# Holding back residual loads until an attention map has been turned: a two-layer hybrid encoder on one core

## The chip, the cores and the metric

The kernel runs on one core of a Trainium2 chip. The metric is the time of one execution in device microseconds (us). Times are medians of a few runs of the same program. The rows shown come from one profiled execution.

## The reference

Two layers over 512 tokens of width 1024, in float32. Each layer computes

```
xn  = RMSNorm(x) * g0
mix = [ A(xn) | B(xn) | C(xn) ] @ w_out        # one input projection, three mixers
h   = x + RMSNorm(mix) * g1
y   = h + RMSNorm( convFFN( RMSNorm(h) * g2 ) ) * g3
```

A is a mixture of dilated window attentions (4 heads), B a bidirectional gated linear recurrence computed in chunks (4 heads), and C is differential attention: 4 heads, each with two query/key maps of 64 dims and values of 128 dims, dense over the sequence; the second softmax is subtracted from the first with a learned weight, and the result goes through an RMSNorm. Queries and keys of A and C get a partial rotation. The convFFN projects to 2 x 2816 columns, runs a convolution of width 3 along the tokens, gates one half with the SiLU of the other and projects back to 1024.

## The kernel before, in words

Each float32 operand of a product is split into a rounded part and a remainder, and a product is three matmuls (`prod`). Weights come in tiles of 128 x 1024 floats (512 KB) into three buffers (`raw`); ScalarE or VectorE makes the rounded part, VectorE the remainder (the subtraction), and only then is the buffer free for the next load. Activations live as four row tiles of 128 tokens, or transposed ("turned") as eight k-slices of 128 features by 512 tokens, again in two parts.

One layer goes: the input projection in chunks, interleaved with the mixers (`mixer`, in the order of `STEPS`); the mixers' results are turned into `xm`, slices 0 to 3 for A and B (`turn_ab`) and slice 4 + h for head h of C (`turn_c`), where head 1 is turned first; the output projection from `xm`; for each row tile the post norm, which adds the residual `x` (`post_norm`), and the second norm, whose result is turned into `xn` (`norm_in`); then the FFN (`ffn`), whose convolution weights stand in `conv`.

For each pair of maps of A and C, `queries_keys` projects queries and keys, multiplies them by cosines and sines on VectorE, lets GpSimd issue four small DMAs that add the swapped rows, splits the result, and lets GpSimd issue twelve DMAs ("moves", 128 KB each, SBUF to SBUF) that put both halves of queries and keys where the score matmuls read them: eight for the queries' two parts and four for the keys, in the order first half, second half.

All loads from HBM (weights, row tiles, norm weight rows, convolution weights) are issued by SyncE, whose queue is in order: an instruction that waits for its buffer holds all that stand behind it. GpSimd issues the moves.

The order of each engine's instructions is made by a planner (`Plan.order`). Every instruction is recorded with its readers and writers; the planner keeps a clock for each engine and, whenever an engine is free, takes the ready instruction with the lowest number, where weight loads and their splits have theirs lowered by 1875 (`AHEAD`). A result is usable on another engine 200 ns after it ends (2000 ns for a DMA). Buffers share their places with others by stage, and an instruction can be taken only when its buffer has a place. What is issued is the resulting order; semaphores on the chip follow from the data that instructions really share. `once` adds views to what the planner takes an instruction to read, and to nothing else:

```python
    def once(self, *views):
        self.needs.extend(views)
        yield
        del self.needs[-len(views):]
```

The planner's prices, in ns for n elements per partition, of VectorE, ScalarE (plus 93 for each view that it takes as scale, bias or accumulator) and DMAs, and what it adds (40 on VectorE, 20 on ScalarE); a DMA keeps SyncE for its price:

```python
            return 68 + n / (1.92 if fast else 0.96) + 61 * scalar
            return (112 if src else 155) + n / 1.4 + 93 * extra + (61 if n > 512 else 0)
        return math.prod(out.shape) * 4 / 350.0
            cost = op.cost + MORE.get(e, 0)
                free[e] = t + (max(50, op.cost) if e == "sync" else 785)
```

Of the kernel before, what the change touches and what calls it, by code (L numbers as in the profile page):

```python
# [21 lines left out]
NT, NK = 4, 8  # L22
# [494 lines left out]
class Trunk:  # L517
# [544 lines left out]
    def layer(self, l, xs):  # L1062
        nc = self.nc
        if l == 0:
            self.first_constants()
            self.xn = self.x_tiles("x%d" % (l % 2))
            rows = [self.t([128, D], "x") for _ in range(NT)]
            with nc.ahead(6 * AHEAD):
                nc.sync.dma_start(rows[0], xs[0])
                g = self.gain_halves()  # L1070
            for t in range(1, NT):
                with nc.ahead((5 if t == 1 else 2) * AHEAD):
                    nc.sync.dma_start(rows[t], xs[t])
            for t in range(NT):
                with nc.ahead((3 if t < 2 else 0) * AHEAD):
                    self.norm_in(rows[t], g, t, self.xn)
            with nc.ahead(-LATER):
                self.constants()
        self.mixer(l)
        self.x = [self.t([128, D], "x") for _ in range(NT)]  # L1080
        g1, g2 = self.gain(l, 1), self.gain(l, 2)
        for t in range(NT):
            nc.sync.dma_start(self.x[t], xs[t])
        self.xn = self.x_tiles("x%d" % (1 - l % 2))
        first = [self.bank("mm") for _ in range(NT)]

        def token(out, q, t, w):
            for i in range(2):
                k = 2 * q + i
                self.prod(out, [z[:, k, t * 128:(t + 1) * 128] for z in self.xm],  # L1090
                          [z[:, i * 512:(i + 1) * 512] for z in w], k == 0, k == NK - 1)

        for q in range(4):
            w = self.weight(l, BASE["out"] + 2 * q)
            for t in range(NT):
                token(first[t], q, t, w)
        ws = [self.weight(l, BASE["out"] + 2 * q + 1) for q in range(4)]
        for t in range(NT):
            second = self.bank("cp")
            for q in range(4):  # L1100
                token(second, q, t, ws[q])
            with nc.ahead(NORM):
                self.post_norm([first[t], second], self.x[t], g1)
                self.norm_in(self.x[t], g2, t, self.xn)
        self.ffn(l)
# [35 lines left out]
    def ffn(self, l):  # L1141
        nc = self.nc
        v = nc.vector
        y = [self.t([128, D], "y") for _ in range(NT)]
        self.conv = self.t([128, 2 * NJ, 4], "conv")
        nc.sync.dma_start(self.conv, self.a["conv"][:, l])
        groups = [(0, 8), (8, 16)]
        jobs = [(a, b, half, q) for a, b in groups for half in range(2) for q in range(a // 2, b // 2)]
        hs = {}
        ps = None  # L1150
        done = 0

        def piece(a, b, half, q):
            nonlocal ps
            first, last = q == a // 2, q == b // 2 - 1
            if first:
                ps = [self.bank("dn") for _ in range(NT)]
            self.down(l, hs, q, half, ps, range(NT), first, last)
            if last:
                for t in range(NT):  # L1160
                    yt = y[t][:, half * 512:(half + 1) * 512]
                    if a == 0:
                        nc.copy(yt, ps[t])
                    else:
                        v.tensor_tensor(yt, ps[t], yt, op=ALU.add)

        start = [[self.bank("mm") for _ in range(2)] for _ in range(2)]
        for lo in (0, 256):
            for j in range(2):
                self.up(l, j, start[j], lo, lo + 256)  # L1170
        for j in range(NJ):
            if j < 2:
                u = start[j]
            else:
                u = [self.bank("mm") for _ in range(2)]
                self.up(l, j, u)
            hs[j] = self.gate(l, j, u)
            if done < len(jobs) and jobs[done][1] <= j:
                piece(*jobs[done])
                done += 1  # L1180
        for job in jobs[done:]:
            piece(*job)
        g1 = self.gain(l, 3)
        last = l == L - 1
        if not last:
            g2 = self.gain(l + 1, 0)
        ws = {(half, q): self.weight(l, BASE["down"] + 2 * q + half, tag="v%d" % (l % 2) if (half, q) == V_TILE else "w")
              for half in range(2) for q in range(8, 11)}
        if not last:
            self.xn = self.x_tiles("x%d" % (1 - l % 2))  # L1190
        for t in range(NT):
            both = [self.bank("cp" if t == 2 else "mm") for _ in range(2)]
            for half in range(2):
                for q in range(8, 11):
                    self.down(l, hs, q, half, [both[half]], (t,), q == 8, q == 10, ws[half, q])
            ys = [y[t][:, half * 512:(half + 1) * 512] for half in range(2)]
            with nc.ahead(NORM):
                for yt, p in zip(ys, both):
                    v.tensor_tensor(yt, p, yt, op=ALU.add)
                self.post_norm(ys, self.x[t], g1)  # L1200
            if last:
                for half in range(2):
                    h = slice(half * 512, (half + 1) * 512)
                    nc.sync.dma_start(self.a["out"][0, t * 128:(t + 1) * 128, h], self.x[t][:, h])
            else:
                nc.sync.dma_start(self.spill[t], self.x[t])
                with nc.ahead(NORM):
                    self.norm_in(self.x[t], g2, t, self.xn)


WB = 5
V_TILE = (1, 10)


# [9 lines left out]
def lay_out(plan, pool, psum):  # L1224
# [6 lines left out]

    rsize, fsize = (64 + 8 * WB) * K, 86 * K
    rtile = pool.tile([128, rsize], F32R, name="rounded")
# [4 lines left out]
    def place(arena, size, at, tags):  # L1238
        for name, n, bufs in tags:
            at = plan.tag(name, arena, at, n, bufs)  # L1240

        assert at <= size, (at, size)
        return at

    base = place(ra, rsize, 0, (("whi", 4 * K, WB), ("wlo", 4 * K, WB)))
    for side in ("0", "1"):
# [58 lines left out]
```

## Time and profile before

| | |
|---|---|
| median of 3 runs | 1390.62 us (1389.17 to 1391.64) |
| the profiled execution | 1389.02 us, with a span of 1387.3 us |
| TensorE's granted clock, mean | 0.998 of full |
| busy share of the span | TensorE 98%, VectorE 69%, ScalarE 50%, GpSimd 12% |
| loads on SyncE's queue | 129.37 MB, 29.2% of the 16 DMA engines' time |
| GpSimd's DMAs | 20.47 MB, 6.4% |

Busy time is summed over the span; the stretch around the change has its own table below. Nearly every instruction is recorded through one helper, so all carry the same line, L514, and are told apart by engine, operation, shapes and place in time. "full" is the float32 area that holds many tiles, "rounded" the area of split operands, "bank" PSUM; w_d, x_d, gains_d and conv_d are the inputs in HBM, "spill" the store of the first layer's result, from which the second layer loads its residual.

### The profile page before, as it was taken

The page shows a single profiled execution, that of the slowest core. Times are in us where ns is not written, and L with a number is a line of the kernel's source. Part 1 is how long each engine was busy: PE and PEld are TensorE (multiplying, and loading weights), DVE is VectorE, ACT ScalarE, POOL GpSimd, SP SyncE. Part 2 cuts the span into 40 slices and gives each one's busy share as a digit, 9 for nine tenths or more (in the row PEclk, how much of TensorE's full clock was granted, in tenths as well). Part 3 has the DMA queues.
Part 4 walks back from the last instruction along what each step waited for, and adds up shares of the span by engine and source line. Part 5 has one row for each costly group of instructions (what it writes and reads, how often), then busy time and mean ns, then how long its engine had stood idle before and what let it go on. Part 6 is the DMA issues. An engine that isn't in the chain of part 4 may idle for free.

```text
span 1387.3 us, 19687 instructions
## 1 busy us (share of the span) xinstructions
PE 1361.5 (98%) x7462; PEld 1165.5 (84%) x7462; DVE 957.4 (69%) x1655; ACT 695.7 (50%) x1171; POOL 160.8 (12%) x263
## 2 busy tenths in 40 slices
PE   8999999999999999999999999999999999999997
PEld 6998889877888888888899888897888888888885
DVE  6789999858765455445768899997586644554374
ACT  4837875645543334323356576756464433343231
POOL 1031332311000000000111132333010000000000
PEclk9999999999999999999999999999999999999999
DMA  7343442623523223223253343355153332332311
GB/s 249 122 112 101 113 112 72 174 75 100 174 92 100 98 91 106 93 94 104 72 179 97 119 117 99 84 145 137 46 158 116 95 103 92 101 97 91 107 62 61
DMA packets 46159, 151.10 MB, mean 109 GB/s; under 512 B 7920, under 2 KB 8432, under 8 KB 46064
## 3 DMA queue, kind: packets, MB, share of 16 engines
q1 hardware_dynamic: 37584, 129.37, 29.2%
q0 software_dynamic: 8480, 20.47, 6.4%
q8 instruction: 59, 0.97, 0.3%
q14 instruction: 36, 0.29, 0.1%
HBM read 125.17 MB, written 4.19 MB: 93 GB/s over the span
## 4 chain that ended last, share of the span: by engine, by line
PE 92%; DVE 4%; issue 1%; ACT 1%; DMA 1%; POOL 1%; DVEq 0%; POOLq 0%; ACTq 0%
PE bank L514 92%; DVE full L514 2%; DVE rounded L514 1%; ACT full L514 1%; POOL full L514 1%; DMA full<-full 0%; ACT rounded L514 0%; DMA full<-gains_d 0%; DVE qz L514 0%; DVEq L1275 0%; POOLq L1275 0%; DVEq L514 0%; POOL ident masks.py:197 0%; ACTq L514 0%; POOLq masks.py:199 0%
## 5 line engine op out<-in xcount | busy, mean ns | idle before, releaser
L514 PE MATMUL bank<-rounded 128*128 128x512 f32 (+1 forms) x5904 | 1218.3, 363 | 2.4 <-DVE rounded L514 1.6
L514 PEld LDWEIGHTS bank<-rounded 128*128 128x128 f32 x5904 | 992.7, 189 | 166.4 <-ACT rounded L514 2.5
L514 DVE TENSOR_TENSOR rounded<-full,rounded 128x1024 fp32r<-128x1024 f32 (+2 forms) x268 | 294.1, 1110 | 210.4 <-ACT rounded L514 204.9
L514 ACT ACTIVATE rounded<-full 128x1024 fp32r<-128x1024 f32 (+2 forms) x241 | 237.3, 987 | 366.3 <-PE bank L514 328.3
L514 ACT ACTIVATE full<-full 128x512 f32<-128x512 f32 (+7 forms) x335 | 183.6, 568 | 108.8 <-DVE full L514 96.2
L514 ACT ACTIVATE full<-bank,full 128x512 f32<-128x512 f32 (+1 forms) x182 | 121.5, 673 | 119.0 <-PE bank L514 78.0
L514 DVE SCALAR_TENSOR_TENSOR full<-bank,full 128x511 f32<-128x511 f32 x176 | 130.4, 747 | 50.9 <-ACT full L514 48.1
L514 DVE TENSOR_TENSOR full<-full 128x256 f32<-128x256 f32 (+2 forms) x265 | 146.7, 573 | 12.5 <-ACT full L514 4.1
L514 POOL TENSOR_TENSOR full<-full,half 128x1 f32<-128x1 f32 (+1 forms) x48 | 45.0, 939 | 903.0 <-DVE full L514 903.0
L514 ACT ACTIVATE full<-bank 128x512 f32<-128x512 f32 (+2 forms) x160 | 89.6, 574 | 42.6 <-PE bank L514 34.4
L514 PE MATMUL bank<-full 128*128 128x128 f32 (+2 forms) x640 | 82.4, 297 | 3.6 <-ACT full L514 3.6
L514 PEld LDWEIGHTS bank<-full 128*128 128x128 f32 (+1 forms) x640 | 72.4, 180 | 15.3 <-ACT full L514 7.3
L514 POOL DMA_DIRECT2D rounded<-full x144 | 75.1, 533 | 50.0 <-ACT full L514 33.4
L514 DVE SCALAR_TENSOR_TENSOR full<-full 128x512 f32<-128x512 f32 (+1 forms) x100 | 71.9, 738 | 10.6 <-POOL full L514 10.0
L514 PE MATMUL bank<-ident,full 128*128 128x128 f32 x464 | 72.1, 279 | 5.3 <-DVE full L514 5.2
L514 POOL DMA_DIRECT2D full<-full x48 | 41.2, 1248 | 258.6 <-DVE full L514 258.6
L514 PEld LDWEIGHTS bank<-ident,full 128*128 128x128 f32 x464 | 56.3, 143 | 17.0 <-DVE full L514 10.4
L514 PE MATMUL bank<-qz,full 128*128 128x128 f32 x448 | 63.4, 282 | 0.6 <-DVE full L514 0.2
L514 PEld LDWEIGHTS bank<-qz,full 128*128 128x128 f32 x448 | 58.0, 190 | 7.1 <-DVE full L514 4.7
L514 DVE TENSOR_TENSOR full<-bank,full 128x512 f32<-128x512 f32 (+1 forms) x56 | 35.9, 648 | 25.4 <-PE bank L514 25.2
L514 DVE TENSOR_TENSOR qz<-full 64x256 f32<-64x256 f32 x112 | 46.6, 416 | 4.8 <-PE bank L514 2.5
L514 DVE TENSOR_REDUCE full<-bank 128x1 f32<-128x512 f32 x64 | 43.7, 685 | 5.5 <-PE bank L514 4.3
(59 smaller groups left out, 369.5 us busy)
## 6 DMA issues: line engine op xcount, KB each, us to landing
full<-w_d SPq DMA_DIRECT2D x204, 512.0 KB, 3.5
rounded<-full POOLq DMA_DIRECT2D x144, 128.0 KB, 4.0
full<-w_d SPq DMA_DIRECT2D x16, 384.0 KB, 3.2
full<-x_d SPq DMA_DIRECT2D x8, 512.0 KB, 4.4
full<-gains_d SPq DMA_DIRECT2D x7, 512.0 KB, 4.6
spill<-full SPq DMA_DIRECT2D x4, 512.0 KB, 2.8
full<-spill SPq DMA_DIRECT2D x4, 512.0 KB, 5.3
out_d<-full SPq DMA_DIRECT2D x8, 256.0 KB, 2.0
```

The lines of the kernel that those rows point to most:

```text
L514: f(*[real(v) for v in op.args], **{k: real(v) for k, v in op.kw.items()})
```

## The change

Two places get a `once`. The loads of two norm weight rows (`g1`, `g2`) and of the four row tiles of the residual are, for the planner, readers of slice 5 of `xm`'s rounded part, which `turn_c` writes for head 1, the second map of kind C. The load of the convolution weights is a reader of the first 128 tokens of `xn`, which `norm_in` writes for the first row tile.

```diff
@@ layer
         self.mixer(l)
         self.x = [self.t([128, D], "x") for _ in range(NT)]
-        g1, g2 = self.gain(l, 1), self.gain(l, 2)
-        for t in range(NT):
-            nc.sync.dma_start(self.x[t], xs[t])
+        with nc.once(self.xm[0][:, LAST_MAP]):
+            g1, g2 = self.gain(l, 1), self.gain(l, 2)
+            for t in range(NT):
+                nc.sync.dma_start(self.x[t], xs[t])
@@ ffn
         self.conv = self.t([128, 2 * NJ, 4], "conv")
-        nc.sync.dma_start(self.conv, self.a["conv"][:, l])
+        with nc.once(self.xn[0][:, :, 0:128]):
+            nc.sync.dma_start(self.conv, self.a["conv"][:, l])
@@
 WB = 5
+LAST_MAP = 5
 V_TILE = (1, 10)
```

## Rows read from the trace of the kernel before

**Rows 1.** The page, parts 1 and 4: busy time, and the chain by engine.
```profile
PE 1361.5 (98%) x7462; PEld 1165.5 (84%) x7462; DVE 957.4 (69%) x1655; ACT 695.7 (50%) x1171; POOL 160.8 (12%) x263
...
PE 92%; DVE 4%; issue 1%; ACT 1%; DMA 1%; POOL 1%; DVEq 0%; POOLq 0%; ACTq 0%
```

**Rows 2.** Busy time by stretch, both layers.
```profile
core 0: us, PE busy (x) PEld busy (x) DVE busy (x) ACT busy (x) POOL busy (x), PEclk, DMA share, GB/s
...
230.00:262.00 32.00, 32.00 (x213) 28.57 (x212) 26.63 (x51) 18.70 (x40) 11.95 (x18) 1.00 0.57 158
262.00:285.00 23.00, 21.14 (x120) 17.41 (x118) 17.54 (x34) 13.76 (x31) 10.53 (x17) 1.00 0.67 186
285.00:330.00 45.00, 44.30 (x226) 36.67 (x226) 28.81 (x54) 23.65 (x55) 5.14 (x7) 1.00 0.16 47
...
944.00:967.00 23.00, 20.88 (x119) 17.15 (x117) 17.28 (x35) 13.76 (x31) 10.54 (x17) 1.00 0.69 185
```

**Rows 3.** SyncE's queue in order of time: start, duration.
```profile
230.55 0.33 SPq L514 DMA_DIRECT2D full<-gains_d  x1
...
245.59 0.33 SPq L514 DMA_DIRECT2D full<-x_d  x1
...
260.64 0.33 SPq L514 DMA_DIRECT2D full<-w_d  x1
261.07 1.60 SPq L514 DMA_DIRECT2D full<-x_d  x2
271.90 25.49 SPq L514 DMA_DIRECT2D full<-w_d  x3
```

**Rows 4.** TensorE in order of time, 280 to 286 us; idle time in brackets.
```profile
280.62 1.16 PE L514 MATMUL bank<-full 128*128 128x128 f32 x8 [1.13 <-ACT full L514]
...
284.25 0.71 PE L514 MATMUL bank<-rounded 128*128 128x512 f32 x2
285.27 2.11 PE L514 MATMUL bank<-rounded 128*128 128x512 f32 x8 [0.31 <-ACT rounded L514]
```

**Rows 5.** ScalarE in order of time, 262 to 287 us.
```profile
268.27 0.69 ACT L514 ACTIVATE rounded<-bank,dnorm 128x512 fp32r<-128x512 f32 x1 [1.26 <-PE bank L514]
...
271.13 0.64 ACT L514 ACTIVATE full<-full 128x512 fp32r<-128x512 f32 x1
```

**Rows 6.** VectorE in order of time, around 270 and 311 us.
```profile
270.65 1.22 DVE L514 TENSOR_TENSOR rounded<-full,rounded 128x1024 fp32r<-128x1024 f32 x1
...
311.50 0.69 DVE L514 TENSOR_TENSOR full<-bank,full 128x512 f32<-128x512 f32 x1 [0.83 <-PE bank L514]
```

**Rows 7.** GpSimd in order of time: issues of the moves.
```profile
272.06 4.17 POOL L514 DMA_DIRECT2D rounded<-full  x8 [3.39 <-ACT full L514]
277.83 2.15 POOL L514 DMA_DIRECT2D rounded<-full  x4 [1.60 <-DMA rounded<-full]
```

**Rows 8.** DMA issues, us to landing: at 164.6, 272.3, 279.0, 204.0 us.
```profile
rounded<-full POOLq DMA_DIRECT2D x1, 128.0 KB, 2.2
...
rounded<-full POOLq DMA_DIRECT2D x1, 128.0 KB, 5.2
...
rounded<-full POOLq DMA_DIRECT2D x1, 128.0 KB, 3.9
...
full<-w_d SPq DMA_DIRECT2D x1, 512.0 KB, 6.8
rounded<-full POOLq DMA_DIRECT2D x1, 128.0 KB, 6.6
```

**Rows 9.** DMA queues (packets, MB, share): 260:265, 273:275 (two), 275:277 us.
```profile
q1 hardware_dynamic: 306, 1.12, 63.5%
...
q1 hardware_dynamic: 108, 0.43, 79.9%
q0 software_dynamic: 3, 0.01, 1.5%
...
q0 software_dynamic: 151, 0.44, 98.9%
```

## Prediction

> **What bounds the kernel now.** The page comes first: TensorE is busy for 98% of the span and the chain that ended last lies on it for 92% [rows 1]. So a change of the order of loads can only lose or win what TensorE idles. The table by stretch then shows where that is, around the loads that the diff moves: from 230 to 262 us TensorE is busy for 32.00 of 32 us; from 262 to 285 us for 21.14 of 23, and in the same place of the second layer for 20.88 of 23 [rows 2]. All that the loads of today could cost is therefore in the 1.86 and 2.12 us of those two stretches or nowhere: while most of them run, TensorE does not wait. The timeline of SyncE's queue then gives the places of the loads [rows 3], the timeline of TensorE the places of its waits [rows 4], and the DMA views what two queues do to each other [rows 8, 9].
>
> **What the diff does to the order.** The wait is in the planner, not in the program: `once` adds a predecessor when the order is worked out, and what is issued has no semaphore for it. So the question is only where SyncE's queue gets each load. Before: one norm row at 230.55 us, the first row tile at 245.59, the other norm row after it, then a weight load at 260.64, two row tiles from 261.07, and weight loads from 271.90 [rows 3]; the last row tile gets its place only when the last head of C is done. The planner charges SyncE 1.5 us for a load and sees some 10 us between weight loads there, so none of these is delayed in its reckoning by more than one such charge; I take the order of TensorE, VectorE, ScalarE and GpSimd to be unchanged, and only SyncE's queue to be dealt anew.
>
> The planner lets the loads go 0.2 us after ScalarE's rounded copy of the second map (that at 268.27 us [rows 5]; its split is the first of the four). It charges 524288 / 350 = 1.50 us of SyncE for each. Behind that copy, by its own formulas, stand one exponential (112 + 512/1.4 + 186 + 20 = 684 ns), the rounding of a weight tile (967 ns), a lag of 200, VectorE's subtraction (1175 ns) and a lag of 200: the next weight load is ready 3.23 us after the copy. Two norm rows keep SyncE until 0.2 + 3.0 = 3.20 us, so the first row tile goes third, by 0.03 us, then the weight load, which has the higher priority, then the second and third row tile. The last one waits for its place as before. The same holds in the second layer, whose stretch is the same [rows 2].
>
> On the chip nothing holds the first three: they follow the weight load of 260.64 at once, from about 261.1 us. But the weight load that is next in the queue waits for its buffer until VectorE's subtraction of 270.65 is done, and goes at 271.90 [rows 3, 6]; **two row tiles of 512 KB each are now queued behind that wait** and go at about 272.3 us. Before, they went 10 us sooner.
>
> **What they meet there.** At 272.06 GpSimd begins to issue twelve moves of 128 KB, eight and then four, the rotated queries and keys of the last map [rows 7]. That map's first score product stands in TensorE's queue at 284.25 us, two matmuls [rows 4], and needs the moves of the first half, of which the last is the eleventh: the third of the four, issued at about 277.83 + 2 x 0.54 = 278.9 and landed 3.9 us later, at 282.8 [rows 7, 8]. So the cover is 284.25 - 282.8 = 1.4 us.
>
> The price of a load in front of the moves, by rows: undisturbed, such a move lands 2.2 us after its issue; the first of these, behind the one weight load of 271.90, took 5.2 [rows 8], 3.0 us more. From 273 to 275 us SyncE's queue has the engines for 79.9% of the time and GpSimd's for 1.5%, and from 275 to 277 GpSimd's has 98.9% [rows 9]: the moves start when the load is through. In those 2 us the load moved 0.43 MB, so 0.524 MB hold the engines for 2 x 0.799 x 0.524/0.43 = 1.95 us; with no moves about, from 260 to 265 us, it is 5 x 0.635 x 0.524/1.12 = 1.49 us [rows 9]. I take 1.95, the row of the same place, and keep 1.49 and 3.0 as ends.
>
> The sum for one layer: two loads, 3.9 us; less the cover of 1.4; less the 0.31 us that TensorE waits just behind, for a ScalarE copy that will be done by then [rows 4]: 2.2 us. Two layers: **4.4 us slower**, with ends 2 x (2.98 - 1.71) = 2.5 and 2 x (6.0 - 1.71) = 8.6 us. Past that point TensorE is full (44.30 of 45 us [rows 2]), so nothing gives the loss back.
>
> [...]
>
> **Parts that I cost at nothing.** The removal of loads from 230 to 256 us: TensorE is full there [rows 2]. The three loads at 261 us instead of two: one load more in front of the four small accumulating moves, after which ScalarE copies at 271.13 with no wait before it [rows 5]; VectorE's and ScalarE's other work hides it, and since the twelve moves queue behind the row tiles anyway it does not add; were the cover gone, it costs one load at most, 1.5 to 1.95 us in each layer. The norm row is first used at 311.50 us [rows 6], 40 us after its load. The convolution weights, now behind the first turned tile of the second norm, go past one weight load and are read first by the gated convolution, tens of us later. Behind the weight load of 271.90, in SyncE's queue, only these two row tiles wait; the weight load after them waits for its own buffer longer than they take to issue.
>
> **The rivals.**
> *Shared engines, no change.* If the engines serve both queues by turns, about half of the two loads' 2.98 to 3.9 us falls in front of the eleventh move: it lands at 284.3 to 284.8 us, past the cover by 0.1 to 0.5 us, of which 0.31 is waited anyway; 0 to 0.4 us in all, 1390.6 to 1391.0. For it: near 204 us a weight load and a move, issued side by side, landed after 6.8 and 6.6 us, both late, so the queues do mix [rows 8]. Against it: the 1.5%.
> *Another order.* The margin of 0.03 us is thin. If the weight load went before all three row tiles, three stand in front: 2 x (5.85 - 1.71) = 8.3 us, 1398.9. If all five loads went before it, none meets the twelve moves, but three more loads than today stand in front of the accumulating ones, 4.5 us less the two that left: some 1.5 to 3 us in each layer before cover, 0 to 2.6 us in all, 1390.6 to 1393.2.
> *Faster.* The moves of the third map run amid the loads of 230 to 256 us. If they set when that map's softmax chain begins, it would end sooner, and the waits of 1.13 us and the like in that chain's tail [rows 4] would shrink: at most 1.86 + 2.12 = 4.0 us, 1386.6. It decides only if the third map's first scores wait for those moves; TensorE's 32.00 of 32 us before 262 speak against it.
> *The change does nothing*: possible only if a planner's dependence does not move the queue; the first case covers its time.
>
> **How the numbers follow.** The forecast has 0.52, another order 0.12 (three in four of it slower), shared engines or nothing 0.24, faster 0.12. A measurement of this kernel tells no less than about 0.2% (2.8 us) from no change. Of the forecast's own range, 2.5 to 8.6, little lies below that. So slower 0.58, same 0.30, faster 0.12. The profiled execution took 1389.02 us, 1.7 beside its span; the sum against it is 1393.4. The median of the runs is 1.6 above it, at 1390.62, so for a median I say 1395.0 us. The likeliest case's own range is 1393.1 to 1399.2; the range that also holds the unchanged case goes from 1389.4 to 1399.0.
>
> **What will show it.** In the changed profile: two norm rows and one row tile at 261 to 262.5 us; two row tiles at 272.2 to 273; the first of the twelve moves landing after 8 us or more; TensorE idle about 2 us just before the last map's first score, and the stretch 262 to 285 us (and its twin) fuller of idle by as much; every engine else in its old order. I am wrong if the row tiles do not stand between 272 and 273 us, if the moves land as soon as before, or if the matmuls before 262 us turn out to be quicker.

## The result, and the profile after

The changed kernel takes 1399.51 us (median of six executions, 1398.02 to 1400.11) against 1390.32 us (six executions beside it, 1389.17 to 1391.64): a ratio of 1.0067, 95% interval 1.0057 to 1.0077. It is slower by 9.2 us. The forecast was 1395.0 with a range to 1399.0, so the sign was right and the size was not. The profiled execution took 1398.02 us, the fastest of its six, with a span of 1396.2; against the profiled one of before (1389.02) that is 9.0 us, and this is the difference that the rows below account for.

Nothing but SyncE's queue differs between the two programs: TensorE, VectorE, ScalarE and GpSimd issue the same instructions in the same order. The page of the kernel after, parts 1, 4 and 5:

```profile
PE 1364.7 (98%) x7462; PEld 1167.6 (84%) x7462; DVE 958.1 (69%) x1655; ACT 696.2 (50%) x1171; POOL 161.1 (12%) x263
...
PE 88%; DVE 4%; issue 3%; DMA 2%; POOL 2%; ACT 1%; DVEq 0%; POOLq 0%; ACTq 0%; SPq 0%
...
L514 PE MATMUL bank<-rounded 128*128 128x512 f32 (+1 forms) x5904 | 1220.8, 364 | 7.9 <-DMA rounded<-full 6.2
```

Beside [rows 1] two things have moved. TensorE's share of the chain fell from 92% to 88%, and the matmuls' idle time, 7.9 us, is now mostly put down to the moves of rotated queries and keys (6.2 us of it). And the same 7462 matmuls are busy for 3.2 us longer (1364.7 against 1361.5): something made matmuls longer, too.

SyncE's queue after, in order of time (start, duration):

```profile
218.99 42.55 SPq L514 DMA_DIRECT2D full<-w_d  x5
261.58 0.90 SPq L514 DMA_DIRECT2D full<-gains_d  x2
262.52 0.43 SPq L514 DMA_DIRECT2D full<-x_d  x1
272.46 0.33 SPq L514 DMA_DIRECT2D full<-w_d  x1
272.83 2.06 SPq L514 DMA_DIRECT2D full<-x_d  x2
281.93 21.96 SPq L514 DMA_DIRECT2D full<-w_d  x2
...
322.14 0.33 SPq L514 DMA_DIRECT2D full<-w_d  x1
322.52 0.42 SPq L514 DMA_DIRECT2D full<-conv_d  x1
```

Against [rows 3]: two norm rows and one row tile follow the weight load near 261 us, and two row tiles now stand behind the one of 272.46.

GpSimd's queue after, the twelve moves of the last map in layer 1:

```profile
272.76 4.18 POOL L514 DMA_DIRECT2D rounded<-full  x8 [3.53 <-ACT full L514]
278.74 1.03 POOL L514 DMA_DIRECT2D rounded<-full  x2 [1.79 <-DMA rounded<-full]
280.06 0.52 POOL L514 DMA_DIRECT2D rounded<-full  x1 [0.29 <-DVE full L514]
283.12 0.52 POOL L514 DMA_DIRECT2D rounded<-full  x1 [2.54 <-DMA rounded<-full]
```

Before, the last four went in one run of 2.15 us from 277.83 [rows 7]. Now the twelfth is issued at 283.12, and what ends the wait is the landing of another move. How long three of these loads and moves took, from the DMA view, each in the stretch in which it is issued (the eleventh move, the weight load of 281.93, the twelfth move):

```profile
rounded<-full POOLq DMA_DIRECT2D x1, 128.0 KB, 7.4
...
full<-w_d SPq DMA_DIRECT2D x1, 512.0 KB, 7.1
...
rounded<-full POOLq DMA_DIRECT2D x1, 128.0 KB, 6.3
```

The eleventh, issued at 280.06, lands 7.4 us later, near 287.5; the twelfth near 289.4, behind the weight load that was issued 1.2 us ahead of it. In [rows 8] the eleventh took 3.9 us.

TensorE after, in order of time, first layer 1, then the same place of layer 2 (idle time before an instruction in brackets):

```profile
281.18 1.16 PE L514 MATMUL bank<-full 128*128 128x128 f32 x8 [1.12 <-ACT full L514]
...
283.46 1.16 PE L514 MATMUL bank<-full 128*128 128x128 f32 x8 [0.69 <-ACT full L514]
...
287.62 1.20 PE L514 MATMUL bank<-rounded 128*128 128x512 f32 x4 [2.57 <-DMA rounded<-full]
289.48 6.93 PE L514 MATMUL bank<-rounded 128*128 128x512 f32 x17 [0.66 <-DMA rounded<-full]
...
975.95 5.04 PE L514 MATMUL bank<-rounded 128*128 128x512 f32 x21 [2.93 <-DMA rounded<-full]
```

The first row is the one of [rows 4] that stood at 280.62: up to there the kernel after is 0.56 us late. Then the last map's first scores wait for the moves, 2.57 us and 0.66 us in layer 1, and 2.93 us in layer 2, where before there was a wait of 0.31 for ScalarE in each. The last thing to see is in the row of 289.48: 17 matmuls take 6.93 us, while 21 of the same kind in layer 2 take 5.04. The table by stretch shows why (last columns: granted clock, DMA share, GB/s):

```profile
core 0: us, PE busy (x) PEld busy (x) DVE busy (x) ACT busy (x) POOL busy (x), PEclk, DMA share, GB/s
262.00:285.00 23.00, 21.19 (x121) 17.56 (x119) 18.19 (x35) 13.89 (x30) 10.55 (x17) 1.00 0.83 222
285.00:330.00 45.00, 41.77 (x202) 34.43 (x202) 23.08 (x44) 19.81 (x46) 3.71 (x5) 0.92 0.19 56
...
289.40:295.20 5.80, 5.72 (x14) 4.47 (x15) 1.45 (x3) 1.31 (x4) 0.85 (x1) 0.50 0.00 1
...
967.00:990.00 23.00, 18.26 (x105) 15.10 (x104) 14.81 (x29) 13.15 (x30) 3.09 (x5) 1.00 0.40 98
```

From 289.4 to 295.2 us the granted clock is 0.50, and TensorE is busy for all but 0.08 us of that stretch: a busy engine at half speed, with no transfer about (DMA share 0.00). In [rows 2] this stretch, 285 to 330 us, had 44.30 us of TensorE at 1.00; now it has 41.77 at 0.92.

The account of the 9.0 us: 0.56 ahead of the place; waits in layer 1, 2.57 + 0.66 - 0.31 = 2.9; waits in layer 2, 2.93 - 0.31 = 2.6; and the clock. For the clock, the same 17 matmuls at full clock took 4.16 us in an experiment below, so 6.93 - 4.16 = 2.8. Together 8.9. The 0.56 us is not the change's: it arises near 82 us, where TensorE waits 0.76 us for VectorE in place of 0.17, long before any load that was moved, and the same program profiled a second time is 0.1 us ahead of the kernel before at this place. So the change's own part of this execution is about 8.4 us.

### The profile page after: what moved, and what is told of

Read it like the earlier page. It is cut to its first block, busy times and chain, and to the rows that moved or that the text cites. A ratio compares the mean times of both kernels' runs of the same rounds, so it can differ in the third digit from the quotient of the medians.

```text
span 1396.2 us, 19688 instructions
## 1 busy us (share of the span) xinstructions
PE 1364.7 (98%) x7462; PEld 1167.6 (84%) x7462; DVE 958.1 (69%) x1655; ACT 696.2 (50%) x1171; POOL 161.1 (12%) x263
## 4 chain that ended last, share of the span: by engine, by line
PE 88%; DVE 4%; issue 3%; DMA 2%; POOL 2%; ACT 1%; DVEq 0%; POOLq 0%; ACTq 0%; SPq 0%
PE bank L514 88%; DVE full L514 2%; DMA rounded<-full 1%; DVE rounded L514 1%; POOL full L514 1%; POOL rounded L514 1%; DMA full<-full 0%; ACT full L514 0%; DMA full<-gains_d 0%; DMA full<-w_d 0%; DVE qz L514 0%; ACT rounded L514 0%; DVEq L1278 0%; POOLq L1278 0%; DVEq L514 0%
```

## The experiments

All times are medians, each beside executions of the kernel before on the same chip.

| version | us | before | ratio, 95% interval |
|---|---|---|---|
| only the convolution weights wait | 1390.11 | 1390.02 | 1.0003, 0.9994 to 1.0012 |
| no row tile behind the late weight load | 1389.25 | 1390.02 | 0.9992, 0.9984 to 1.0001 |
| one behind it | 1393.84 | 1390.02 | 1.0028, 1.0017 to 1.0040 |
| the same program again | 1392.14 | 1389.53 | 1.0020, 1.0010 to 1.0030 |
| two behind it (the change) | 1399.51 | 1390.32 | 1.0067, 1.0057 to 1.0077 |
| the change again | 1402.36 | 1390.33 | 1.0081, 1.0067 to 1.0095 |
| three behind it | 1404.36 | 1390.02 | 1.0100, 1.0086 to 1.0114 |
| all held one map longer | 1390.46 | 1389.53 | 1.0005, 0.9996 to 1.0014 |
| all five ahead of the late weight load | 1395.68 | 1389.53 | 1.0043, 1.0031 to 1.0056 |
| the change with fillers, planned | 1393.87 | 1389.53 | 1.0033, 1.0021 to 1.0046 |
| before with fillers, planned | 1390.64 | 1389.53 | 1.0009, 1.0000 to 1.0018 |
| the change with fillers, order kept | 1397.52 | 1390.33 | 1.0052, 1.0039 to 1.0064 |
| before with fillers, order kept | 1394.96 | 1390.33 | 1.0032, 1.0019 to 1.0044 |

"The late weight load" is the one of 271.9 us in [rows 3].

**Which of the two gates, and how many row tiles.** One gate alone (the edit is against the change):

```diff
-        with nc.once(self.xm[0][:, LAST_MAP]):
-            g1, g2 = self.gain(l, 1), self.gain(l, 2)
-            for t in range(NT):
-                nc.sync.dma_start(self.x[t], xs[t])
+        g1, g2 = self.gain(l, 1), self.gain(l, 2)
+        for t in range(NT):
+            nc.sync.dma_start(self.x[t], xs[t])
```

> Only the load of the convolution weights is held back; norm rows and row tiles stand where they stood. Theory (the two row tiles behind the weight load of 272 us make the twelve moves late, and TensorE's clock falls after the wait): no part of the 9.2 us is here, 1390.3 us, within 1. Rival (the later convolution load, which stands between weight loads of the output projection and the FFN, costs something): up to a few us over 1390.3, with waits for weight loads on ScalarE after 322 us.

The convolution gate alone costs nothing that can be told (1.0003). So the loss is looked for in the other gate. There, the number of norm rows inside it sets how many row tiles get past the late weight load: none with both outside, one with `g1` outside, and three with both inside but the gate on the remainder of the slice, which is written later than its rounded part.

```diff
         # rows_only
+        g1, g2 = self.gain(l, 1), self.gain(l, 2)
         with nc.once(self.xm[0][:, LAST_MAP]):
-            g1, g2 = self.gain(l, 1), self.gain(l, 2)
             for t in range(NT):
         # one_behind
+        g1 = self.gain(l, 1)
         with nc.once(self.xm[0][:, LAST_MAP]):
-            g1, g2 = self.gain(l, 1), self.gain(l, 2)
+            g2 = self.gain(l, 2)
         # three_behind
-        with nc.once(self.xm[0][:, LAST_MAP]):
+        with nc.once(self.xm[1][:, LAST_MAP]):
```

> Norm rows load as before; the four row tiles are held back. By the planner's prices three of them go right behind the weight load of 261 us and none behind that of 272 us. Theory: the twelve moves land as in the kernel before, 1390.3 to 1391.5 us, granted clock 1.00 from 285 to 300 us. Rival (the burst at 261 us, one load more than before, delays the four accumulating moves, and that is the loss): 1394 us or more.

> As the change, but the first norm row loads as before, so that one row tile instead of two stands behind the weight load of 272 us. Theory: the eleventh move, 4.1 us late with two loads, comes some 2 us late; less the cover of 1.4 and the 0.3 that is waited anyway, 0.3 us per layer, and no fall of the clock: 1390.5 to 1392 us. Rival (each load costs its share of the 9.2 us, with no cover): 1394.9 us.

> As the change, but held back until the remainder of the same map is written, some 1 us later in the planner, so that all three row tiles stand behind the weight load of 272 us. Theory: 6.1 us late less 1.7, 4.4 us of waiting in each layer, 8.9 in all, and a fall of the clock of about 2.7 us in both layers: 1402 to 1405 us; without the clock's part 1399.2. Rival (a load beyond the second adds nothing, since the moves have begun by then): 1399.5 us, as the change.

None behind: as before (1.0). That the loads wait, or that three stand at 262 us, costs nothing; that they stand behind the late weight load does. Three behind came as expected. With one behind, the loss was expected to be hidden by the cover, and 3.8 us were measured: a price by the load, less a fixed cover, doesn't hold. TensorE with three behind, then with one, both in layer 1:

```profile
292.05 7.17 PE L514 MATMUL bank<-rounded 128*128 128x512 f32 x21 [6.08 <-DMA rounded<-full]
```

```profile
289.67 6.66 PE L514 MATMUL bank<-rounded 128*128 128x512 f32 x21 [3.22 <-DMA rounded<-full]
```

One load made TensorE wait 3.22 us here; in layer 2 of the same execution the wait was the usual 0.31 for ScalarE. The difference is in GpSimd's queue. In layer 1:

```profile
280.05 0.52 POOL L514 DMA_DIRECT2D rounded<-full  x1 [1.83 <-DMA rounded<-full]
280.80 0.52 POOL L514 DMA_DIRECT2D rounded<-full  x1 [0.23 <-DMA rounded<-full]
283.51 1.03 POOL L514 DMA_DIRECT2D rounded<-full  x2 [2.19 <-DVE rounded L514]
```

The eleventh move goes out only at 283.51, after the third has landed at 282.96 (no more than eight moves are on their way at once, here and in every trace of this study). The row puts the wait down to VectorE, whose last result before it came at 283.3; but the ninth move, too, goes out 0.54 us after the landing that it waits for (279.51 and 280.05), so the landing alone explains the time. The next weight load had gone at 283.32 and lands 5.9 us later; the move takes 6.0. Both of three-behind's waits (6.08, and 5.48 in layer 2) are followed by a stretch at a granted clock of 0.5.

**Is it the next weight load?** The kernel with one row tile behind, with that load held, by `once`, for the last map's moves (lines left out at the dots):

```diff
+            if index == HELD and self.last_qk:
+                held.enter_context(nc.once(*self.last_qk))
...
                 nc.sync.dma_start(raw, self.a["w"][l, index, :, 0:n])
```

> One row tile behind the late weight load, as in the version with one norm row loaded early, and now the next weight load on SyncE's queue (second of the feed-forward's first group, issued at 283.32 us there) waits in each layer until the twelve moves have landed; the order of the four compute engines is the same. Theory, that the loss of the version with one row behind (1393.8 us) came from this weight load, which was issued 0.2 us before the eleventh move and landed in front of it: the eleventh move is still issued at about 283.5 us, since at most eight are in flight, but lands some 4 us later, at 287.4 in place of 289.5 us; the score waits under 1 us in place of 3.22 us, TensorE keeps its clock behind it, and the time is 1390.3 to 1391.6 us. Rival, that one row's load ahead of the moves costs this by itself, by delaying them: the wait stays near 3 us with the stretch at half clock behind it, and the time stays at 1393 to 1394.5 us. Held too long, the weight load could make the engine that rounds it wait; that would show as a wait of VectorE or ScalarE on a DMA behind 290 us.

This experiment didn't do what its expectation says. `once` puts no wait into the program; it only moves a load in SyncE's queue, and this one has no neighbour there to change places with. What ran is the program with one row tile behind, unchanged: every engine and SyncE's queue have the same order in both traces. So it tells nothing for or against holding the load, but it is a second sample of the same program, and a useful one: its nine executions go from 1390.38 to 1395.03 us, and the profiled one is the fastest. There, in layer 1:

```profile
278.44 1.69 POOL L514 DMA_DIRECT2D rounded<-full  x3 [1.95 <-DMA rounded<-full]
281.36 0.52 POOL L514 DMA_DIRECT2D rounded<-full  x1 [1.23 <-DMA rounded<-full]
```

```profile
285.35 5.05 PE L514 MATMUL bank<-rounded 128*128 128x512 f32 x21 [0.60 <-DMA rounded<-full]
```

All twelve moves are out by 281.36, ahead of the weight load at 281.63; the score waits 0.60 us, the clock stays up, and the execution costs 5.4 us less than the profiled one above (1395.82). Not all of this is the race: 1.75 us lie ahead of 84 us, where TensorE ran at a granted clock of 0.50 from 20.9 to 24.2 us in the dearer execution and at 1.00 in the other (the table by stretch of each):

```profile
20.90:24.20 3.30, 3.30 (x18) 3.30 (x17) 2.88 (x5) 1.92 (x3) 0.00 (x0) 0.50 0.77 232
...
20.90:24.20 3.30, 3.30 (x30) 3.30 (x30) 3.30 (x5) 2.28 (x4) 0.00 (x0) 1.00 0.88 239
```

The rest, some 3.7 us, lies at and behind this place. Same instructions, another outcome of the race between the last moves and the next weight load: the third move landed 7.8 us after its issue in the one and 5.6 in the other, and with that the eleventh fell behind the load or ahead of it. Why the third took longer isn't shown, and that a real wait on the weight load would mend the kernel wasn't tried.

**Held longer, or sent ahead.**

```diff
         # next_map
-LAST_MAP = 5
+LAST_MAP = 4
         # five_ahead
         with nc.once(self.xm[0][:, LAST_MAP]):
-            g1, g2 = self.gain(l, 1), self.gain(l, 2)
-            for t in range(NT):
-                nc.sync.dma_start(self.x[t], xs[t])
+            with nc.ahead(AHEAD):
+                g1, g2 = self.gain(l, 1), self.gain(l, 2)
+                for t in range(NT):
+                    nc.sync.dma_start(self.x[t], xs[t])
```

> As the change, but held back until the next map (head 0 of C) is turned: all five loads then follow the weight load that the kernel before issues at 281.4 us, when the last of the twelve moves has been issued. Theory: the moves land as in the kernel before and nothing else needs these loads before 311 us: 1390.3 us, within 1. Rival (holding the loads back costs in itself, by the late convolution weights or by loads that meet the output projection's weights): 1394 us or more.

> As the change, but the held loads get the priority of weight loads, so that all five go before the weight load of 272 us, right behind that of 261 us. Theory: no load but that one weight load is in front of the twelve moves; the four accumulating moves stand behind three loads more than before and may come up to 3 us late, of which the cover takes 1.4: 1390.3 to 1394 us, with no fall of the clock. Rival (the number of held loads is what counts, not their place): 1399.5 us.

With a longer hold all five loads go behind the weight load of about 281 us, when the twelve moves are out: no loss. With the loads sent ahead none stands between the late weight load and the moves, and the scores wait for no move (0.31 us, for ScalarE). The kernel still loses 6.2 us, more than expected, in part at another place. TensorE in that version, both layers:

```profile
276.63 1.16 PE L514 MATMUL bank<-full 128*128 128x128 f32 x8 [1.77 <-ACT full L514]
...
960.62 1.16 PE L514 MATMUL bank<-full 128*128 128x128 f32 x8 [1.96 <-ACT full L514]
```

These waits are new. Their chain begins at the four small accumulating moves, which now meet five loads and hold back the queries and keys that the twelve moves wait for (the twelve start at 276.39 in place of 272.06 [rows 7]; 2.1 us of that had been lost by 84 us). The two waits are 3.7 us. Two stretches at a granted clock of 0.50 add to this execution's time, 21.7 to 25.0 us and 1035.4 to 1038.7 us; the trace of the longer hold, which loses nothing, has one like the first, and the cause of the second is open. So the place near 262 us has room for the three loads of the change, not for five.

**Is it the waiting, or its clock?** Eight matmuls that need none of the moves are put just ahead of the last map's first score in each layer, so that TensorE has work while the moves land. In the first pair, whose edit is shown, the planner knows of them and the order of other work shifts too; in the second the order is kept and they are only inserted when it is issued.

```diff
                 p = self.bank(tag)
+                if (h, t, m) == (3, 0, 0):
+                    for _ in range(FILL):
+                        nc.tensor.matmul(p, self.xm[0][:, 4, 0:128], self.xm[0][:, 4], start=True, stop=True)
                 self.scores(p, qk, m, t)
```

> As the change, with eight more matmuls of 512 columns on TensorE just before the last map's first score in each layer; their results are overwritten by it, and the output is unchanged. At full clock they take 8 x 0.227 = 1.8 us and stand where TensorE waits for the moves. Theory (about 2.7 us or more of the loss is TensorE at half clock after its wait): the granted clock stays at 1.00 from 285 to 300 us, and the kernel, with 16 matmuls more, is faster than the change: 1396 to 1398 us. Rival (all of the loss is waiting, or the slow matmuls come from something else): 1399.5 to 1401 us.

> The same eight matmuls in each layer of the kernel before; all engines but SyncE have the same order as in fill_after. Nothing is waited for there, so they cost their own time and the wait for what they read: 2 x (1.8 + 0.5) = 4.6 us, about 1395 us by both theories. The difference to fill_after is then what the late moves cost without a fall of the clock: 1 to 3 us by the theory, 5 us or more by the rival.

> As the change, with the eight matmuls of 512 columns put before the last map's first score when the order is already made, so that every engine has the order of the change and TensorE only the 16 matmuls more; their results are overwritten. In the trace of the change TensorE waits 2.57 + 0.66 us there in the first layer and 2.93 in the second, and then runs 13 matmuls at 427 instead of 227 ns in the first. Theory (two parts, waiting and clock): no stretch at half clock after the scores, and 1396 to 1397.5 us, some 2 to 3 faster than the change beside it. Rival (the slow matmuls are not the clock, or cost nothing that counts): 1399.5 us or more.

> The same matmuls in the same way in the kernel before, whose order is otherwise kept. Theory: they wait for what they read and then run, 2 x (0.5 + 1.8) = 4.6 us, 1394 to 1395 us. With fill_before, whose planner knew of the matmuls and which took 1.1 us more than the kernel before, this tells what the new order there gave back: about 3.5 us if this run comes out as expected, nothing if it comes out near 1391.

> The change itself, beside the two others on one chip: 1399 to 1400 us, granted clock 0.993 to 0.996 in its executions; a trace in which the clock falls in no layer would be some 3 us shorter than one in which it falls in one.

Planned, the change with fillers is 3.2 us slower than before with fillers, in place of 9.2 for the change without fillers on another chip. Both came out quicker than expected, so the planner's new order gave something back. With the order kept, 2.6 us (1397.52 against 1394.96), in place of 12.0 for the change without fillers on the same chip (1402.36 against 1390.33). The changed kernel is 4.8 us quicker with sixteen matmuls more, while the same matmuls cost the kernel before 4.6. TensorE in the change with fillers, order kept, layer 1 and then layer 2:

```profile
286.73 2.12 PE L514 MATMUL bank<-rounded 128*128 128x512 f32 x8 [0.78 <-ACT rounded L516]
288.68 1.17 PE L516 MATMUL bank<-rounded 128*128 128x512 f32 x4
290.37 4.16 PE L516 MATMUL bank<-rounded 128*128 128x512 f32 x17 [0.53 <-DMA rounded<-full]
...
974.60 5.03 PE L516 MATMUL bank<-rounded 128*128 128x512 f32 x21 [0.53 <-DMA rounded<-full]
```

The fillers, in the first row, wait 0.78 us for what they read and cover most of the wait for the moves (0.53 us of it is left in each layer), and the clock stays at 1.00 in all of 285 to 300 and 967 to 990 us. In the change again, without fillers, TensorE's rows in the same two places are:

```profile
289.71 6.51 PE L514 MATMUL bank<-rounded 128*128 128x512 f32 x21 [5.32 <-DMA rounded<-full]
...
975.70 6.55 PE L514 MATMUL bank<-rounded 128*128 128x512 f32 x21 [2.86 <-DMA rounded<-full]
```

and its clock by stretch in layer 1 (in layer 2 it is 0.50 as well, from 975.5 to 978.9 us):

```profile
289.40:292.80 3.40, 3.09 (x7) 2.48 (x8) 0.92 (x3) 0.78 (x2) 1.01 (x1) 0.50 0.01 2
```

Both waits are followed by 21 matmuls at 1.6 us over the 4.93 us that 21 take undisturbed (in the kernel before with fillers, order kept, in the same place). Waits beyond those of before: 5.32 + 2.86 - 0.62 = 7.6; clock: 1.58 + 1.62 = 3.2; 10.8 us in all, against 1399.57 - 1389.02 = 10.6 for this profiled execution. The wait of 5.32 us has the cause seen with one row tile behind: the eleventh move goes out at 281.67, 0.4 us after the next weight load (281.26), and lands 7.9 us later. So about two thirds of the loss in the two profiled executions of the change is waiting and one third is the clock behind it. The median, 1402.36, is above the 1399 to 1400 expected; three of the five executions took 1402.4 us or more, and none of these was profiled. The fillers take away both at once, and these runs don't part the two; the parting is that of the trace, where the same matmuls are longer at a granted clock of 0.5.

## What the prediction had right, and the step that failed

**The order of the queues: right.** Two norm rows and one row tile behind the weight load near 261 us, the late weight load before the other two by the 0.03 us of the planner's reckoning, two row tiles at 272.83, every other engine as before. The rival *another order* fell with it; the two versions that make its orders, three behind and five ahead, came to 1404.4 and 1395.7 where it had 1398.9 and 1390.6 to 1393.2. Both cost more than the rival had for them.

**The cause: right.** It is the row tiles behind the late weight load, ahead of the moves: with none behind, by either way, the loss is gone (0.9992, 1.0005). Loads gone from 230 to 256 us, the third load at 262 us, and the convolution weights cost nothing, as said.

**How late the moves are: right in size, in part by luck.** From the first move's issue to the landing of the eleventh it was 282.8 - 272.06 = 10.7 us [rows 7, 8] and is 287.5 - 272.76 = 14.7: 4.0 us more, where two loads at 1.95 made 3.9. But a third load is in the 4.0: from 285 to 287 us, just before the eleventh lands, the weight load of 281.93, issued after it, has 66.2% of the engines. The prediction had nothing for it, and how much of the delay is its isn't shown. And the picture behind the price held for the first load at most. These are the queues of the kernel after, from 273 to 275, from 275 to 282 and from 285 to 287 us:

```profile
q1 hardware_dynamic: 87, 0.36, 78.7%
...
q1 hardware_dynamic: 325, 1.17, 62.8%
q0 software_dynamic: 235, 0.67, 39.2%
...
q1 hardware_dynamic: 77, 0.32, 66.2%
```

From 273 to 275 SyncE's queue has 78.7% and GpSimd's has no packet, much as in [rows 9]. From then on both move at once, with 62.8 and 39.2% from 275 to 282 us. The rows from 273 to 275 don't speak against that, though the prediction read those of before so. A move that meets no load, issued at 164.48 us in the kernel before, puts its first packet on the engines 1.1 us after its issue; by that one move the first move here, issued at 272.76, would be there at about 273.9, and its first packet comes at 275.1. So an estimated 1.2 us were lost behind the load that had begun (1.5 us in the kernel before, where the move of 272.06 has its first packet at 274.7). How the engines choose between the two queues, no run shows. The rival *shared engines* took half of the row tiles to fall behind the eleventh move, and so nearly no loss. The queues did share, and the loss came all the same: the eleventh move has ten others ahead of it that share the engines with the row tiles, and by the time it lands, near 287.5 us, both row tiles have long been through (landed near 281.2 and 285.0).

**The wait: mis-sized, 2.2 us in each layer against 2.9 and 2.6, and 5.0 and 2.5 in the change again.** The 2.57 us of layer 1 are what the prediction has for this wait, 3.9 less the cover of 1.4. It then took off 0.31 us for a wait behind it that would be gone. In layer 1 another took its place, 0.66 us for the twelfth move. That one is late by 5.4 us, more than the loads' price, because it waited until 283.12 for the fourth to land and found the weight load of 281.93 ahead of it. The 1.60 us of [rows 7] already are a move's wait for a move; the prediction did not ask what it becomes when moves land later. In layer 1 of the change again the same happened to the eleventh.

**The step that failed: "Past that point TensorE is full, so nothing gives the loss back".** It takes the loss to be the waiting alone, at a constant speed of TensorE. But the speed changed behind the waits: TensorE ran 5.8 us at a granted clock of 0.50 in the profiled execution, which cost 2.8 us, and in the change again 1.6 us in each layer. The sum of 4.4 us was to be 5.5 for the waits and 2.8 for the clock in that one, and 7.6 and 3.2 in the other. The prediction had no rival for it, since no row of before in the stretches that it read showed a clock other than 1.00.

In the traces the clock is at 0.50 behind the waits of layer 1 of the kernel after (2.57 and 0.66 us) and of both layers of the change again (5.32 and 2.86 us); in layer 2 of the kernel after, it is at 1.00 behind a wait of 2.93 us. Why it falls, no run shows.

**The cover.** 1.4 us were taken as a fixed sum that one load would not use up. With one row tile behind, executions of one and the same program went from 1390.38 to 1396.66 us: in the two that were profiled, the cover holds or not as the last moves go out before or after the next weight load.

**What stays open.** Which wait is followed by the lower clock and which is not: 2.86 us was, 2.93 us was not. Why the change took 1399.5 us beside one set of executions and 1402.4 beside another. And whether the next weight load, held by a real wait, would take the loss of one row tile away; its part is read from two executions of one program and not from a change made to it.

## What to carry to other kernels

A load's place in a queue is to be judged by what starts next on the other queues, not by when its data is needed: here the row tiles are read 40 us later and the harm is done to twelve moves that start with them (the eleventh landed 4.0 us later). Where a delay goes into a wait of an engine that is otherwise full, count the wait, then look at what the engine's clock does behind it (here 0.50 for 5.8 us, which cost 2.8 us), and at whether a limit on transfers under way (here eight of GpSimd's, by the program's semaphores) pushes the last of them behind the next load. A cover is worth what it is worth in the worst order of the transfers that race for it; executions that spread more than those of before (here 1390.4 to 1396.7 against 1388.3 to 1392.0) can be a sign that it is used up.

## What the runs showed of the hardware beyond that

TensorE's granted clock in this one-core kernel falls behind some of its waits: in layer 1 of the kernel after it is 0.50 from 289.4 to 295.2 us, after waits of 1.12, 0.69, 2.57 and 0.66 within 10 us. Seventeen matmuls of 512 columns then take 6.93 us in place of 4.16 (the change with fillers, order kept). At this place of the two layers it fell behind last waits of 2.86, 3.22, 5.32, 5.48 and 6.08 us, and not behind one of 2.93. With eight matmuls put into the wait, 2.1 us by their row, it stayed at 1.00 in both layers.

The same is seen near 20 us, where TensorE waits for VectorE in every version, in some executions longer than in others: in the six traces with a wait of 2.06 to 2.30 us there the clock is at 0.50 for some 3.4 us behind it, and in the eight with 1.33 to 1.94 us it stays at 1.00. In the trace with one row tile behind, 18 matmuls run there in 3.30 us, and 30 in the same program's other trace, which is 1.75 us ahead by 84 us; so it is worth a look before two profiled executions are set against each other.

In none of the fourteen traces, with 193 transfers of GpSimd in each, were more than eight of these between issue and landing; the ninth and later of a series wait for an earlier one (1.60 us in [rows 7], 2.54 us for the twelfth in layer 1 of the kernel after). In the traces the moves carry eight semaphores in turn, and the ninth waits on that of the first; so this is how the program is built, and no limit of the chip is shown by it.

With a load issued on SyncE's queue 0.3 us ahead of it, the first move had its first packet on the engines 2.4 us after its issue in place of 1.1, while loads issued after that one shared the engines with the moves from 275 us on.
